# Two of three merge gates by one level of Strassen's scheme, in a decoder layer with fp32 split into two fp32r halves

## The chip, the cores and the metric

One core of a Trainium2 chip. The metric is the device time of one execution in microseconds; lower is better. Engines: TensorE (PE, its weight loads PEld), VectorE (DVE), ScalarE (ACT), GpSimd (POOL), SyncE (SP), and 16 DMA engines.

## The reference, cut to what matters

```
h = rms_norm(x, norm_g)                                  # x: 256 tokens x 1024
(qa, ka, va, ga, ub, vb, gb, qc, gc, ma, mb, mc) = split_cols(h @ w_in, IN_SPLITS)
out_a = moba_attention(rope(qa), rope(ka), va) * silu(ga)          # 6 heads x 128
out_b = gmlp_spatial_gate(ub, vb, ...) * silu(gb)                  # 6 groups x 128
out_c = memory_cross_attention(qc, rms_norm(mem), w_mem_kv) * silu(gc)   # 4 heads x 128
y = (sigmoid(ma) * (out_a @ w_branch_a) + sigmoid(mb) * (out_b @ w_branch_b)
     + sigmoid(mc) * (out_c @ w_branch_c))               # ma, mb, mc: 256 x 1024 each
return rms_norm(x + y @ w_out, final_norm_g)
```

All is fp32. Each of `ma`, `mb`, `mc` is a product of 256x1024 by 1024x1024.

## The kernel before

Every fp32 operand of a matmul is split into two fp32r halves, hi (ScalarE, a copy) and lo = value - hi (VectorE), and a product is three passes: hi hi, hi lo, lo hi (`mm3`).

The weights come as one stream of pieces of 128x2048 (1 MB), loaded by SP into `raw`; half a piece is a chunk. `split(c)` makes chunk c's hi and lo (128x1024 each, four buffers each), three chunks ahead of its use. The loop at the end runs over the chunks in one order: 12 `vvb` (value and gMLP columns), 24 of queries, keys, `ub` and `ga`, 4 `qc`, 4 `mk`, 4 `mv`, 4 `gc`, 6 `gb`, 24 `sig` (the gates: two halves of 512 columns for each of the three, four chunks a half), 16 `br` (branch projections), 8 `out`. A `fea` chunk is 24 matmuls of 256 columns with the weights stationary; a `tok`, `br` or `out` chunk is 12 of 512 columns with the activations stationary. A `sig` half goes from PSUM through ScalarE's sigmoid into `sig0`, `sig1`.

Between the chunks stand units (`U.add`): pieces of the attentions, the norms, the gMLP. `U.slot` takes a unit when those that it follows are done and its costs (PE, DVE, ACT, POOL) fit into the chunk's room. The engines' queues are filled in this written order, and each engine works its own queue from the front.

PSUM has two tags of four banks, `acc` and `aux`. `mm_br` multiplies each branch's accumulators with its gates and adds them up; `y_split` transposes the sum and splits it for the output projection. In the tables below h and `nh`/`nl` are the normalized x, transposed, as hi and lo halves (128 x 8 x 256).

Of the kernel before, what the change touches and what calls it, by code (L numbers as in the profile page):

```python
# [81 lines left out]
def tile_hybrid_layer(ctx: ExitStack, tc: tile.TileContext, xw, memT, mem, x, fin_g, ln_g, w, w_sp, b_sp, rope, out):  # L82
# [14 lines left out]
    def bank():  # L97
        return psum.tile([128, 512], F32, name="aux", tag="aux", bufs=4)

    def acc_bank():  # L100
        return psum.tile([128, 512], F32, name="acc", tag="acc", bufs=4)
# [8 lines left out]
    RAW, SPL, LEAD = 3, 4, 3  # L110
# [167 lines left out]

    def mm3(p, s_hi, s_lo, m_hi, m_lo, first, last):
        nc.tensor.matmul(p, s_hi, m_hi, start=first, stop=False)  # L280
        nc.tensor.matmul(p, s_hi, m_lo, start=False, stop=False)  # L281
        nc.tensor.matmul(p, s_lo, m_hi, start=False, stop=last)  # L282

# [10 lines left out]
    def mm_tok(c):  # L294
# [3 lines left out]
        if k0 == 0:  # L298

            acc[name, o] = [bank(), bank()] if o == 1024 else [acc_bank(), acc_bank()]  # L300
        for i in range(2):
# [14 lines left out]
        if k0 + 2 == KD and name == "vvb":
            U.add(f"ev{o}", lambda: evict_v(o), after=["xrms"], cost=(0, 0, 1.2, 0), gap=1, first=True)
        elif k0 + 2 == KD and name == "sig":
            for t in range(2):
# [2 lines left out]
                nc.scalar.activation(V[f"sig{t}"][:, o, :], acc[name, o][t], AF.Sigmoid)  # L322
# [27 lines left out]
    def mm_fea(c):  # L350
# [559 lines left out]
```

## Time and profile before

| what | value |
|---|---|
| three runs | 332.37, 330.72, 332.83 us (median 332.37) |
| profiled execution, span from the first to the last instruction | 330.5 us (the page gives no other time of it) |
| instructions | 5066 |
| TensorE busy | 322.3 us, 98% |
| VectorE, ScalarE, GpSimd busy | 223.1, 191.7, 39.7 us |
| DMA | 62.91 MB, 190 GB/s in the mean |

A row of a group reads: line, engine, operation, output<-inputs, shapes, count | busy us, mean ns of one | idle us before them and who ended it. A row of the timeline reads: start us, duration us, engine, line, operation. Matmuls overlap, so the distance between starts is their pace.

### The profile page before, as it was taken

What the parts mean: (1) busy time and instruction counts of PE and PEld (TensorE: products, weight loads), DVE (VectorE), ACT (ScalarE), POOL (GpSimd) and SP (SyncE); (2) the same over time, 40 slices, a digit from 0 to 9 for tenths busy, and PEclk for the clock granted to TensorE, in tenths of its full rate; (3) what the DMA queues carried; (4) which work ended last, traced back from release to release, by engine and by line L of the source; (5) the groups of instructions that cost most, each with busy time, mean ns of one, the idle gap of its engine ahead of it and who ended that gap; (6) DMA issues with size and microseconds to landing.
All of it is one profiled execution on the core that took longest, in us unless ns stands there. A gap on an engine that the chain in (4) does not pass through costs nothing.

```text
span 330.5 us, 5066 instructions
## 1 busy us (share of the span) xinstructions
PE 322.3 (98%) x1998; PEld 290.0 (88%) x1998; DVE 223.1 (68%) x339; ACT 191.7 (58%) x315; POOL 39.7 (12%) x42
## 2 busy tenths in 40 slices
PE   7999999999999999999999999999999999999992
PEld 4888899999999999988999988888888888888882
DVE  5864969978957898678694755354435469768553
ACT  5777769566785666547864466535553633533432
POOL 0007310000001090100026530000000000000022
PEclk9999999999999999999999999999999999999997
DMA  7998884554433371643655263646465565563003
GB/s 276 393 420 313 313 346 144 225 183 167 164 139 130 127 255 41 225 138 117 242 190 211 70 236 136 248 153 229 140 243 172 209 184 198 143 238 129 0 4 124
DMA packets 11159, 62.91 MB, mean 190 GB/s; under 512 B 1248, under 2 KB 2400, under 8 KB 4608
## 3 DMA queue, kind: packets, MB, share of 16 engines
q1 hardware_dynamic: 10560, 61.62, 51.8%
q10 hardware_dynamic: 576, 0.98, 0.8%
q8 instruction: 15, 0.25, 0.3%
q14 instruction: 8, 0.07, 0.1%
HBM read 61.55 MB, written 1.05 MB: 189 GB/s over the span
## 4 chain that ended last, share of the span: by engine, by line
PE 96%; DMA 1%; DVE 1%; ACT 0%; issue 0%; DVEq 0%; SPq 0%
PE acc L280 26%; PE acc L281 26%; PE acc L282 26%; PE acc L309 4%; PE aux L280 3%; PE aux L281 3%; PE aux L282 3%; PE aux L472 2%; DMA st<-in_xw_dram 1%; PE aux L641 1%; PE aux L512 0%; PE aux L545 0%; PE aux L226 0%; DVE xk L755 0%; DVE fb L770 0%; ACT jk L760 0%
## 5 line engine op out<-in xcount | busy, mean ns | idle before, releaser
L134 DVE TENSOR_TENSOR lo<-raw,hi 128x1024 fp32r<-128x1024 f32 x102 | 127.7, 1254 | 72.6 <-ACT hi L130 68.4
L130 ACT ACTIVATE hi<-raw 128x1024 fp32r<-128x1024 f32 x102 | 107.7, 1057 | 55.5 <-PE acc L282 47.4
L280 PE MATMUL acc<-nh,hi 128*128 128x256 f32 x304 | 86.7, 285 | 0.0
L282 PE MATMUL acc<-nh,lo 128*128 128x256 f32 x304 | 86.0, 283 | 0.0
L281 PE MATMUL acc<-nl,hi 128*128 128x256 f32 x304 | 86.0, 283 | 0.0
L281 PEld LDWEIGHTS acc<-nl,hi 128*128 128x128 f32 x304 | 58.3, 192 | 0.0
L280 PEld LDWEIGHTS acc<-nh,hi 128*128 128x128 f32 x304 | 58.3, 192 | 0.0
L282 PEld LDWEIGHTS acc<-nh,lo 128*128 128x128 f32 x304 | 58.3, 192 | 0.0
L280 PE MATMUL acc<-hi,nh 128*128 128x512 f32 x96 | 37.5, 390 | 0.0
L282 PE MATMUL acc<-hi,nl 128*128 128x512 f32 x96 | 37.4, 389 | 0.0
L281 PE MATMUL acc<-lo,nh 128*128 128x512 f32 x96 | 37.4, 389 | 0.0
L282 PEld LDWEIGHTS acc<-hi,nl 128*128 128x128 f32 x96 | 18.0, 188 | 3.8
L280 PEld LDWEIGHTS acc<-hi,nh 128*128 128x128 f32 x96 | 18.0, 188 | 3.7
L281 PEld LDWEIGHTS acc<-lo,nh 128*128 128x128 f32 x96 | 18.0, 188 | 3.7
L764 POOL TENSOR_TENSOR xk<-xk,fing 128x512 f32<-128x512 f32 (+1 forms) x4 | 4.0, 1010 | 126.6 <-ACT jk L760 126.6
L650 POOL TENSOR_TENSOR qk<-qk,ga 128x512 f32<-128x512 f32 x3 | 4.0, 1334 | 71.5 <-ACT qk L546 71.5
L421 POOL TENSOR_TENSOR st<-st,bc 128x256 f32<-128x256 f32 x8 | 7.9, 1026 | 25.6 <-DMA trig<-in_rope_dram 25.6
L322 ACT ACTIVATE sig<-acc 128x512 f32<-128x512 f32 x12 | 7.1, 598 | 5.3 <-PE acc L282 4.9
L280 PE MATMUL acc<-hi,ah 128*128 128x512 f32 x24 | 9.4, 393 | 0.0
L282 PE MATMUL acc<-hi,al 128*128 128x512 f32 x24 | 9.4, 390 | 0.0
L281 PE MATMUL acc<-lo,ah 128*128 128x512 f32 x24 | 9.3, 389 | 0.0
L282 PE MATMUL acc<-hi,obl 128*128 128x512 f32 x24 | 9.3, 389 | 0.0
(210 smaller groups left out, 592.3 us busy)
## 6 DMA issues: line engine op xcount, KB each, us to landing
raw<-in_w_dram SPq DMA_DIRECT2D x50, 1024.0 KB, 4.8
st<-in_xw_dram SPq DMA_DIRECT2D x6, 384.0 KB, 6.3
raw<-in_w_dram SPq DMA_DIRECT2D x2, 512.0 KB, 8.6
xk<-in_x_dram SPq DMA_DIRECT2D x1, 1024.0 KB, 11.9
mt<-in_memT_dram SPq DMA_DIRECT2D x2, 512.0 KB, 7.0
mm<-in_mem_dram SPq DMA_DIRECT2D x2, 512.0 KB, 8.6
fing<-in_fin_g_dram SPq DMA_DIRECT2D x1, 512.0 KB, 5.7
out_dram<-xk ACTq DMA_DIRECT2D x2, 224.0 KB, 2.6
```

Source lines behind the costliest of these rows:

```text
L130: nc.scalar.activation(hi[c][:, a:b], raw[c // 2][:, o + a:o + b], AF.Copy)
L134: nc.vector.tensor_tensor(lo[c][:, a:b], raw[c // 2][:, o + a:o + b], hi[c][:, a:b].bitcast(F32), OP.subtract)
L280: nc.tensor.matmul(p, s_hi, m_hi, start=first, stop=False)
L281: nc.tensor.matmul(p, s_hi, m_lo, start=False, stop=False)
L282: nc.tensor.matmul(p, s_lo, m_hi, start=False, stop=last)
L309: nc.tensor.matmul(acc[name, o][t][:, a:b], src[:, k, tsl(t)], wt[c][:, i * 512 + a:i * 512 + b], start=k + n == 0, stop=k == KD - 1 and n ...
L322: nc.scalar.activation(V[f"sig{t}"][:, o, :], acc[name, o][t], AF.Sigmoid)
L421: U.add(f"nm{k}", lambda k=k: nc.gpsimd.tensor_tensor(x_k(k), x_k(k), bc["x"], OP.mult), after=["xrms"], gap=1)
L472: nc.tensor.transpose(p[:, hsl(j)], src, ident)
L641: nc.tensor.matmul(pv[:, a, t, :], V["vb"][:, t, hsl(g)], wsp[:, g, :], start=True, stop=True)
L650: nc.gpsimd.tensor_tensor(src, src, g, OP.mult)
L764: nc.gpsimd.tensor_tensor(z, z, V["fing"][:, a:b], OP.mult)
```

## The change

**The gates a and b.** With h and the weight cut into quarters (tokens by 128, inner and outer columns by 512), each gate is seven products of quarter size in place of eight (Winograd's form of Strassen's scheme): p1 and p2 on quarters of h, p5, p6, p7, p3 on four sums of quarters (`quad_sums`, GpSimd; split into `sh` and `sl` by `quad_hi`, `quad_lo`), p4 on a quarter again. A product is 12 matmuls of 512 columns and splits two tiles of 128x1024. The sums of weight quarters are made by DMA: `base` holds quarter 0, p1 uses it, then quarters 1, 3 and 2 are added to it by accumulating transfers from GpSimd's queue, and p5, p6 and p4 use it; p2, p3 and p7 come through the stream, p7 with one add. The results add up in PSUM (banks x and y, held over several products) and in the gates' tiles. Gate c is computed as before. The sigmoid becomes a tanh of half the value, with the factors folded into `mm_br` and `y_split`.

**The order.** The 14 products stand among 22 ordinary chunks (6 `gb`, the 8 `sig` of gate c, 6 `br` of branch a and 2 of b), by `TURN`. A product counts as two tiles of the four that may be split ahead.

**Banks.** Eight tags of one bank each; `bank()` takes the longest unused one that isn't held, `let_go` gives a held one back.

**Passes.** In a chunk all hi passes stand first and the lo passes follow (`mm_group`, `mm_fea`).

Besides, `raw` has four buffers (before three), x is loaded a second time for the residual, and several tiles share other slots of SBUF.

```diff
-    RAW, SPL, LEAD = 3, 4, 3
+    RAW, SPL = 4, 4
-    for g in range(6):
-        chunks += [("tok", "sig", g, 2 * i) for i in range(4)]
-    for half in range(2):
-        chunks += [("br", half, i) for i in range(KD)]
+    for half in range(2):
+        chunks += [("tok", "sig", half, 2 * i) for i in range(4)]
+    for br, half, n in (("a", 0, HA), ("a", 1, HA), ("b", 0, GB), ("c", 0, HC), ("b", 1, GB), ("c", 1, HC)):
+        chunks += [("br", br, half, k) for k in range(0, n, 2)]
...
+    QUARTER = {"p1": 0, "p2": 2, "p3": 3, "p7": 1}
+    TURN = (0, 0, "p1", 0, "p2", 0, 0, "p5", 0, "p3", 0, 0, "p6", 0, "p7", 0, 0, "p4")
+    n_plain = chunks.index(("fea", "gb", 0))
+    steps, nf = [("F", c) for c in range(n_plain)], n_plain
+    for u in range(2):
+        for p in TURN:
+            steps.append(("S", u, p) if p else ("F", nf))
+            nf += not p
+    ROOM = {"F": (1.3, 1.4, 1.35, 2.5), "S": (1.3, 0.3, 0.5, 2.5)}
...
+    def mm_group(parts):
+        for p, s_hi, s_lo, m_hi, _, first, _ in parts:
+            nc.tensor.matmul(p, s_hi, m_hi, start=first, stop=False)
+            nc.tensor.matmul(p, s_lo, m_hi, start=False, stop=False)
+        for p, s_hi, _, _, m_lo, _, last in parts:
+            nc.tensor.matmul(p, s_hi, m_lo, start=False, stop=last)
...
         for k in range(KD):
-            mm3(p, hi[c][:, hsl(k)], lo[c][:, hsl(k)], sh[:, k, :], sl[:, k, :], k == 0, k == KD - 1)
+            nc.tensor.matmul(p, hi[c][:, hsl(k)], sh[:, k, :], start=k == 0, stop=False)
+            nc.tensor.matmul(p, hi[c][:, hsl(k)], sl[:, k, :], start=False, stop=False)
+        for k in range(KD):
+            nc.tensor.matmul(p, lo[c][:, hsl(k)], sh[:, k, :], start=False, stop=k == KD - 1)
...
+    def quad_sums():
+        V["sx"] = sx = act.tile([128, 4, 4, 128], F32, name="sx", tag="base")
...
+        tt(s1, part(h, 1, 0), part(h, 1, 1), OP.subtract)
+        tt(s1, s1, part(l, 1, 0), OP.add)
...
+    U.add("quads", quad_sums, after=[f"nxl{k}" for k in range(KD)] + ["lna0", "lna1", "mk1"], gap=0)
...
+    def load_base(u):
+        base[u] = act.tile([128, PIECE], F32, name="base", tag="base")
+        nc.gpsimd.dma_start(base[u], quarter(u, 0))
+    def add_quarter(t, u, q):
+        nc.gpsimd.dma_start(t, quarter(u, q), accum_op=OP.add)
...
+    def fast_out(u, p):
...
+        b, i, op = {"p1": (x, 0, None), "p2": (z, 0, OP.add), "p5": (y, 3, None), "p3": (y, 1, None),
+                    "p6": (x, 1, OP.subtract), "p7": (x, 3, OP.subtract), "p4": (x, 2, None)}[p]
+        if p == "p4":
+            tanh_gate(u, 2, x)
+            let_go(("x", u))
+        elif op is None:
+            nc.scalar.activation(GATE[u][i], b, AF.Copy)
...
+        else:
+            nc.vector.tensor_tensor(GATE[u][i], GATE[u][i], b, op)
+            U.add(f"h{u}{i}", lambda: tanh_gate(u, i, GATE[u][i]), cost=(0, 0, 0.65, 0), first=True)
...
+        then = {"p1": 1, "p5": 3, "p6": 2}.get(p)
+        if then is not None:
+            add_quarter(base[u], u, then)
+        if p == "p4" and u < 1:
+            load_base(u + 1)
```

What stands where, at the three places that matter. First TensorE. Before, where the `sig` chunks begin (`mix` is the gMLP's last unit, `wsp,vb`; then per block of 512 columns the passes hi hi, lo hi, hi lo as weight,activation):

```order
L641 MATMUL aux<-wsp,vb 128x128 x4
L280 MATMUL acc<-hi,nh 128x512
L281 MATMUL acc<-lo,nh 128x512
L282 MATMUL acc<-hi,nl 128x512
L280 MATMUL acc<-hi,nh 128x512
L281 MATMUL acc<-lo,nh 128x512
L282 MATMUL acc<-hi,nl 128x512
```

Now the first product, p1 of gate a (L833, whole: two tiles of six matmuls), which stands between the lo passes of gb1 and a transposition of the cross attention:

```order
L393 MATMUL acc<-nh,lo 128x256 x8
L833 MATMUL acc<-hi,nh 128x512
L833 MATMUL acc<-hi,nl 128x512
L833 MATMUL acc<-hi,nh 128x512
L833 MATMUL acc<-hi,nl 128x512
L833 MATMUL acc<-lo,nh 128x512 x2
L833 MATMUL acc<-hi,nh 128x512
L833 MATMUL acc<-hi,nl 128x512
L833 MATMUL acc<-hi,nh 128x512
L833 MATMUL acc<-hi,nl 128x512
L833 MATMUL acc<-lo,nh 128x512 x2
L510 MATMUL acc<-ident,p 128x128 x4
```

A product takes a chunk's place with one chunk's matmuls, and a lo tile is first read by the fifth matmul of its six. 748 matmuls of 512 columns have become 724.

Second, GpSimd from the attention's gating (`qk<-qk,ga`) through the gMLP (`ub`). Before:

```order
L650 TENSOR_TENSOR qk<-qk,ga 128x2x256 x2
L650 TENSOR_TENSOR oc<-oc,gc 128x512
L386 TENSOR_TENSOR ub<-ub,sq 128x256 x2
L689 TENSOR_TENSOR ub<-ub,mt_2192 128x512
L386 TENSOR_TENSOR ub<-ub,sq 128x256
L650 TENSOR_TENSOR oc<-oc,gc 128x512
```

Now, from the last gating of attention on (ahead of it stand the 11 sums, `sx`; L805 is the load of a base, L808 an add):

```order
L688 TENSOR_TENSOR qk<-qk,ga 128x2x256
L805 DMA base<-in_w_dram 128x2048
L688 TENSOR_TENSOR oc<-oc,gc 128x512
L808 DMA base<-in_w_dram 128x2048
L424 TENSOR_TENSOR ub<-ub,sq 128x256 x3
L727 TENSOR_TENSOR ub<-ub,mt_2266 128x512
L808 DMA base<-in_w_dram 128x2048
L424 TENSOR_TENSOR ub<-ub,sq 128x256
L688 TENSOR_TENSOR oc<-oc,gc 128x512
```

An add waits in this queue for the add before it and for VectorE's lo of the tile it adds to; the gatings behind it wait with it.

Third, ScalarE from p6's tiles to p4's (L955 splits a product's tile, L144 a chunk's, `sg` is gate a, `base` and `raw` the tiles split); before, this engine's queue held only chunk splits and sigmoids there:

```order
L955 ACTIVATE hi<-base 128x1024 x2
L144 ACTIVATE hi<-raw 128x1024
L752 ACTIVATE sg_2197<-sg_2197 128x512
L955 ACTIVATE hi<-raw 128x1024 x2
L144 ACTIVATE hi<-raw 128x1024 x2
L752 ACTIVATE sg_2197<-sg_2197 128x512
L955 ACTIVATE hi<-base 128x1024 x2
```

p7's two tiles stand behind the tanh of p6's result (the first L752), p4's behind the tanh of p7's.

More of the change, by code (lines that the diff above doesn't have):

```diff
@@ L95, in slot_tile, with bank, let_go @@
         return V[name]
[L97 to L101, printed above, removed]
+    turn, held = list(range(8)), set()
+    def bank(hold=None):
+        i = next(i for i in turn if i not in held)
+        turn.remove(i)
+        turn.append(i)
+        if hold:
+            held.add(i)
+            V["bank", hold] = i
+        return psum.tile([128, 512], F32, name="acc", tag=f"b{i}")
+    acc_bank = bank
+    def let_go(hold):
+        i = V.pop(("bank", hold))
+        held.discard(i)
+        turn.remove(i)
+        turn.append(i)
     def tsl(t):
@@ L298, in mm_tok @@
         if k0 == 0:
-            acc[name, o] = [bank(), bank()] if o == 1024 else [acc_bank(), acc_bank()]
+            acc[name, o] = [bank((name, o, t) if name != "vvb" else None) for t in range(2)]
         for i in range(2):
@@ new lines, in tile_hybrid_layer, with load_ring @@
+    ring = []
+    for i, stp in enumerate(steps):
+        if stp[0] == "F" and stp[1] % 2 == 1 and stp[1] // 2 >= 2:
+            ring.append((i, stp[1] // 2))
+        elif stp[0] == "S" and stp[2] in ("p2", "p3", "p7"):
+            ring.append((i, stp))
+    ring.sort(key=lambda r: r[0])
+    n_loaded = [2]
+    def load_ring(upto):
+        while n_loaded[0] < len(ring) and ring[max(0, n_loaded[0] - RAW + 1)][0] <= upto:
+            _, what = ring[n_loaded[0]]
+            n_loaded[0] += 1
+            if isinstance(what, int):
+                load(what)
+            else:
+                raw[what] = wts.tile([128, PIECE], F32, name="raw", tag="raw", bufs=RAW)
+                nc.sync.dma_start(raw[what], quarter(what[1], QUARTER[what[2]]))
@@ new lines, in tile_hybrid_layer @@
+    nxt = 4
+    last = at["F", n_br + 4 - 1]
+    for i, stp in enumerate(steps[:last + 1]):
+        now[0] = i
+        U.room = ROOM[stp[0]]
+        U.slot(i, False)
+        while nxt < len(steps) and sum(tiles_of(x) for x in steps[i:nxt + 1]) <= SPL:
+            split_step(steps[nxt])
+            load_ring(nxt)
+            nxt += 1
+        for j in range(i, min(i + 8, len(steps))):
+            nx = steps[j]
+            if nx[0] == "S" and nx[2] == "p7" and nx not in cq and nx in raw and at[nx] - i <= 6:
+                cq[nx] = True
+                add_quarter(raw[nx], nx[1], 3)
+        if stp[0] == "S":
+            mm_fast(*stp[1:])
+            fast_out(*stp[1:])
+        else:
+            c = stp[1]
+            kind = chunks[c][0]
+            if kind == "tok":
+                mm_tok(c)
+            elif kind == "fea":
+                mm_fea(c)
+            elif kind == "br":
+                mm_br(c)
+            else:
+                mm_out(c, 0)
+                for a, b in (((0, 256), (256, 512)) if chunks[c][1] else ((0, 512),)):
+                    mm_out(c, 1, a, b)
+            U.done[f"c{c}"] = i
+        U.slot(i, True)
```

208 lines of the change are left out of this document (144 added, 64 removed).

## The prediction

> **What bounds the kernel now.** I read the page's head first, then the chain of work that ended last, then TensorE's own waits, and last the busy time by stretches.
>
> ```profile
> span 330.5 us, 5066 instructions
> PE 322.3 (98%) x1998; PEld 290.0 (88%) x1998; DVE 223.1 (68%) x339; ACT 191.7 (58%) x315; POOL 39.7 (12%) x42
> PEclk9999999999999999999999999999999999999997
> PE 96%; DMA 1%; DVE 1%; ACT 0%; issue 0%; DVEq 0%; SPq 0%
> ```
>
> TensorE is busy for 98% of the span at an undiminished clock, and 96% of the chain is its own work. A busy PE may still hide short holes, so the waits of that engine alone come next:
>
> ```profile
> PE aux L193 <- DVE warm L183: 1.2, 1, 1.2
> PE acc L309 <- ACT hi L243: 0.6, 2, 0.3
> ```
>
> Both belong to the first microseconds. From there to the last matmul TensorE never waits for a split, a load or a bank. Two things follow. What leaves TensorE shortens the kernel at the matmul's own pace; and letting the lo passes follow the hi passes cannot gain anything by itself, since no lo is waited for now. It can only widen a margin.
>
> **The pace of what goes.** Four starts from the sig chunks, which the change rewrites (start, duration):
>
> ```profile
> 202.84 0.39 PE L280 MATMUL acc<-hi,nh 128*128 128x512 f32 x1
> 203.06 0.39 PE L281 MATMUL acc<-lo,nh 128*128 128x512 f32 x1
> 203.29 0.39 PE L282 MATMUL acc<-hi,nl 128*128 128x512 f32 x1
> ...
> 209.86 0.39 PE L281 MATMUL acc<-lo,nh 128*128 128x512 f32 x1
> ```
>
> Starts are what count, not the 0.39 us. Between the first and the last of these rows are 31 starts in 7.02 us: 0.2265 us each. The step is 0.22 or 0.23 whether the stationary tile is the one of the row before (L280 to L281) or another one (L281 to L282), so the new order of passes should cost and gain nothing here.
>
> Two gates now take 2 x 8 chunks x 12 matmuls = 192; as 2 x 7 products x 12 they take 168. Everything else on TensorE keeps its number: 1144 of 256 columns and 78 of 128 in both programs, 748 of 512 before and 724 after. **Saved: 24 x 0.2265 = 5.4 us**, the most that this change can bring.
>
> **What it puts on VectorE and ScalarE.** Fourteen products split 28 tiles of 1024 columns where sixteen chunks split 16: 12 more on each engine. Results add 3 VectorE adds per gate and 3 more ScalarE copies or tanhs per gate (7 for 4); the four sums need 4 conversions and 4 subtractions; one more table load stands among the gb chunks.
>
> ```profile
> L134 DVE TENSOR_TENSOR lo<-raw,hi 128x1024 fp32r<-128x1024 f32 x102 | 127.7, 1254 | 72.6 <-ACT hi L130 68.4 <-PE acc L281 3.3
> L130 ACT ACTIVATE hi<-raw 128x1024 fp32r<-128x1024 f32 x102 | 107.7, 1057 | 55.5 <-PE acc L282 47.4 <-PE aux L282 5.6 <-DMA raw<-in_w_dram 2.4
> L322 ACT ACTIVATE sig<-acc 128x512 f32<-128x512 f32 x12 | 7.1, 598 | 5.3 <-PE acc L282 4.9
> L731 DVE TENSOR_TENSOR sig<-acc,sig 128x512 f32<-128x512 f32 x12 | 8.0, 683 | 0.0
> L484 ACT ACT_TABLE_LOAD x3 | 3.8, 1283 | 0.0
> 174.00:280.00 106.00, 106.00 (x539) 90.73 (x539) 56.91 (x57) 52.71 (x63) 11.62 (x10) 1.00 0.53 187
> ```
>
> The last row is the stretch from the first gb chunk to the middle of the branches (columns: length, busy us of PE, PEld, DVE, ACT, POOL, clock, DMA share, GB/s). VectorE gets 12 x 1.254 + 6 x 0.683 = 19.1 us on top of 56.9, ScalarE 12 x 1.057 + 6 x 0.598 + 1.283 = 17.6 us on top of 52.7. In the 101 us that remain this is 75% and 70%: there is room on the average. The room is thin where a product follows a product's result. p7's hi stands on ScalarE behind a tanh, which waits for VectorE's subtraction of p6. From p6's end: 0.683 + 0.598 + 1.057 = 2.34 us to the first hi tile, 1.254 more to its lo, 3.59. TensorE has one ordinary chunk meanwhile, 12 x 0.2265 = 2.72, and wants the lo four matmuls later, at 3.62. It just fits; hence I put 0.1 to 0.3 us on each of such places (p2 and p7 of both gates), together 0.5. Were the lo still wanted by the second matmul, as in the old order, the same place would cost 0.7: here the widened margin is used.
>
> **The sums on GpSimd.** The sums of hi and lo quarters are 11 tensor_tensor of 128x512 on POOL. They wait only for tiles that are long there, so they run where POOL comes free, right behind its second gating of attention, far ahead of the chunk that plans them:
>
> ```profile
> 123.19 1.31 POOL L650 TENSOR_TENSOR qk<-qk,ga 128x512 f32<-128x512 f32 x1
> 139.12 1.41 POOL L650 TENSOR_TENSOR qk<-qk,ga 128x512 f32<-128x512 f32 x1 [14.62 <-ACT qk L546]
> 136.61 0.42 DVE L288 TENSOR_TENSOR mkl<-sq,cx 128x256 fp32r<-128x256 f32 x1
> 139.60 1.21 DVE L288 TENSOR_TENSOR mkl<-sq,cx 128x256 fp32r<-128x256 f32 x1
> 185.68 1.29 POOL L689 TENSOR_TENSOR ub<-ub,mt 128x512 f32<-128x512 f32 x1 [0.54 <-DVE mt L646]
> 185.83 2.23 DVE L134 TENSOR_TENSOR lo<-raw,hi 128x1024 fp32r<-128x1024 f32 x1 [0.29 <-ACT hi L130]
> 192.10 1.22 DVE L134 TENSOR_TENSOR lo<-raw,hi 128x1024 fp32r<-128x1024 f32 x1
> 127.00:160.00 33.00, 33.00 (x235) 30.86 (x234) 26.11 (x50) 20.97 (x47) 1.41 (x1) 1.00 0.47 160
> ```
>
> The same VectorE instruction takes 0.42 alone and 1.21 beside a GpSimd one, 1.22 alone and 2.23 beside one: it ends as if it had begun when GpSimd's ended. So 11 x 1.29 = 14.2 us of sums run from about 124.5 to 140 or 150, in the stretch where VectorE has 33.0 - 26.1 = 6.9 us of air, less 4 x 0.68 = 2.7 for the new lo halves: 4.2. The two delayed rows lost 0.79 and 1.01 us; at one such loss for half of the sums, 11 x 0.9 / 2 = 5.0. What the air doesn't take, the lead of the splits takes:
>
> ```profile
> 0.00:133.30 133.30, 49.12 (x40) 1.00 0.62 229
> 0.00:164.20 164.20, 59.00 (x49) 1.00 0.59 216
> 133.29 0.41 DVE L371 TENSOR_TENSOR sq<-acc,bc 128x256 f32<-128x256 f32 x1
> 165.26 0.38 ACT L382 ACTIVATE gc<-acc 128x256 f32<-128x256 f32 x1
> ```
>
> The first two rows count finished splits (chunk 4 is the first). At 133.3, when chunk 40 (mk0) is evicted, chunk 43 is split: three ahead. At 165.26, when chunk 50 (gc2) is evicted, it is chunk 52: only two, some 4 us before it is wanted. So a delay of 5 us should vanish in 4.2 of air and 4 of lead. Bounds: 0 at the low end; at the high end all eleven cost VectorE a full 1.29, and 14.2 - 4.2 - 4 = 6.0 us reach TensorE. I take 0.5.
>
> The Trainium skill, "SBUF — State Buffer", section Who interferes with whom, has this as a rule: a VectorE instruction with two SBUF inputs and a GpSimd one that reads SBUF share a read interface, and the later one blocks fully. The rows above agree (2.23 against 1.22). By it as a worst case, every sum blocking, the 6.0 us hold and the gain is gone; by the share seen in the trace, 0.5.
>
> **The accumulating transfers.** A gate's base tile is loaded, and three times a quarter is added to it by DMA from GpSimd's queue; p7's tile gets one such add. No row shows an accumulating transfer. The nearest:
>
> ```profile
> raw<-in_w_dram SPq DMA_DIRECT2D x50, 1024.0 KB, 4.8
> xk<-in_x_dram SPq DMA_DIRECT2D x1, 1024.0 KB, 11.9
> ```
>
> A plain 1 MB lands in 4.8 us in the steady part, in 11.9 in the crowded start. An add must read what it adds to: I take twice 4.8, 9.6 us, with 4.8 and twice 11.9 = 23.8 as ends. The time there is: the add waits for the split of the product that used the tile, and the next one is split five steps later (p1, p5, p6, p4 are five apart). That is 5 x 2.72 = 13.6 us less the two splits themselves (2 x 1.057 + 1.254 = 3.4): 10.2 until ScalarE would wait, and two steps less one hi (5.4 - 1.1) more, about 14.5, until TensorE would. At 9.6 it is hidden. From p4 to the next gate's p1 are three steps and a plain load: 4.8 until ScalarE waits, 9 until TensorE does, for 4.8. Load on the queues: the stretch moves 11 MB of ordinary pieces and 16 quarters, eight of them adds. With 8 more for the adds' second read that is 35 x 1.05 = 36.7 MB in 101 us, 363 GB/s; 187 GB/s made a share of 0.53, so this is 1.03, full, and without the second reads 0.79. Each of six adds into a base may be late at times; I take no stall, by the nearer row, and leave it as the great risk.
>
> The Trainium skill, "DMA: Bandwidth & Descriptors", section Bandwidth, gives 6.15 us for 1 MB issued from GpSimd; twice that, an estimate, is 12.3 us, and by it TensorE still waits for none.
>
> **Sum.** -5.4 (matmuls) + 0.5 (thin places) + 0.5 (sums) + 0 (adds) = -4.4 us on the span of 330.5: 326.1. The page gives no time of this execution beyond its span; the three runs lie between 330.72 and 332.83, and their median is 1.9 above the span. I keep that: 332.4 - 4.4 = **328.0 us**, 1.3% faster.
>
> **Rivals.** *The sums eat it*: VectorE falls behind before the first product and, with two splits per product, can't catch up. For it speaks the 2.23 row, against it the 4.2 us of air. With 2 to 6 us of stalls: 329 to 333, within 1% of now. *The adds are too slow*: beyond 14.5 us from issue to landing every base add stops TensorE, six times. At 15.4 the gain is gone (6 x 0.9), at 18 it is -4.4 + 6 x 3.5 = +16.6, 349 us; at the bound of 23.8, 384. For it speaks the share near full, against it that plain loads at a share of 0.53 still land in 4.8. *The change doesn't do what it says*: the saved matmuls might run at another pace, as the twelve of a product go into one bank with alternating stationary tiles. The equal steps of 0.22 and 0.23 speak against it; 168 x 0.01 = 1.7 us at most, 329.7.
>
> **Chances.** Forecast with up to 2 us of further stalls (325.3 to 329): 0.55. Gain eaten, by sums, thin places or pace (329 to 335.7): 0.25. Adds or anything else beyond: 0.20. About 1% is what a measurement of this kernel can tell from no change. The range takes in the first two cases: its low end is the fastest run less the whole saving, 330.7 - 5.4 = 325.3; its high end 335.
>
> **What would show it.** Right: TensorE's waits still hold only the start; 24 matmuls of 512 columns fewer at 0.2265; adds landing in under 14 us. The sums: rows of lo splits near 2.2 us between 124 and 150. Wrong: TensorE waiting for ScalarE's or VectorE's splits of base tiles, which in turn wait for the DMA queue of GpSimd; or many lo waits from 150 to 180.

## The result, and the profile after

The changed kernel takes 335.73 us in the median (334.19 to 336.45, four runs), the kernel before 331.56 beside it: a ratio of 1.0105, 95% interval 1.0059 to 1.015 (ratios here are worked out from the single runs; the two medians alone would give 1.0126). It is 1% slower, where 328.0 us, 1.3% faster, had been forecast. In the ratios of the experiments below one slow run each of runs 10 and 17 is left out, while the medians keep it. The profiled run took 335.84 us.

The page of the changed kernel (span; busy time of each engine; the chain that ended last):

```profile
span 334.1 us, 5145 instructions
PE 321.2 (96%) x1974; PEld 287.3 (86%) x1974; DVE 251.6 (75%) x361; ACT 206.9 (62%) x338; POOL 66.0 (20%) x62
PE 69%; DVE 16%; ACT 8%; issue 3%; DMA 1%; POOL 1%; DVEq 0%; SPq 0%; ACTq 0%; POOLq 0%
```

TensorE has less to do and a longer span. What it waited for (us in total, times, longest us), the waits of the first microseconds set aside (L207, 1.3, and L342, 0.5):

```profile
PE acc L510 <- DVE p L533: 2.4, 3, 1.2
PE acc L393 <- DVE lo L148: 1.1, 1, 1.1
PE acc L833 <- ACT hi L955: 0.9, 1, 0.9
```

Three waits in the middle of the program, none of which stood in the profile before, and their places by windows (length, then busy us of PE, PEld, DVE, ACT, POOL, clock, DMA share, GB/s):

```profile
120.00:140.00 20.00, 17.84 (x136) 17.45 (x135) 16.97 (x29) 9.66 (x23) 19.53 (x12) 0.91 0.39 143
133.00:136.40 3.40, 3.40 (x19) 3.40 (x18) 3.40 (x6) 1.08 (x2) 3.32 (x3) 0.51 0.69 246
170.00:200.00 30.00, 29.73 (x221) 27.97 (x220) 24.73 (x28) 21.01 (x35) 8.54 (x9) 1.00 0.56 161
200.00:240.00 40.00, 37.90 (x180) 31.19 (x179) 29.80 (x27) 23.90 (x30) 9.97 (x9) 1.00 0.90 274
```

Before, TensorE was busy for the whole of the first, third and fourth of these. The first, before:

```profile
120.00:140.00 20.00, 20.00 (x169) 19.94 (x169) 15.67 (x31) 11.29 (x27) 5.38 (x4) 1.00 0.47 159
```

Two places carry the loss: 120 to 140 us, long before the first product, where GpSimd is busy for 19.53 of 20 us, and 200 to 240 us, among the products of gate a.

To count it whole, take the time from each matmul's start to the next beyond the pace of its kind (0.2266, 0.1195 and 0.061 us for 512, 256 and 128 columns), and sum it by stretch. I call this the loss.

| stretch, us | before | after |
|---|---|---|
| 0 to 10 | 4.14 | 4.79 |
| 10 to 120 | 2.10 | 2.19 |
| 120 to 150 | 0.97 | 4.75 |
| 150 to 170 | 0.66 | 0.46 |
| 170 to 200 | 1.28 | 1.94 |
| 200 to 240 | 0.01 | 3.41 |
| 240 to the end | 0.90 | 1.37 |
| start of the last matmul | 323.87 | 327.28 |

The losses grow by 8.85 us. The saved matmuls, 24 x 0.2266, take 5.44 off; what is left is the 3.41 us by which the last matmul starts later.

**120 to 150 us.** The timeline (start, us, what, idle before and its releaser), from GpSimd, VectorE and TensorE:

```profile
125.20 1.34 POOL L764 TENSOR_TENSOR sx<-nh 128x512 f32<-128x512 f32 x1
126.62 2.16 POOL L765 TENSOR_TENSOR sx<-sx,nl 128x512 f32<-128x512 f32 x1
...
142.05 1.35 POOL L773 TENSOR_TENSOR sx<-sx,nl 128x512 f32<-128x512 f32 x1
125.31 2.31 DVE L148 TENSOR_TENSOR lo<-raw,hi 128x1024 fp32r<-128x1024 f32 x1
130.06 1.56 DVE L533 TENSOR_SCALAR p<-p,rc 128x128 f32<-128x128 f32 x2
130.40 0.33 PE L510 MATMUL acc<-ident,p 128*128 128x128 f32 x1 [1.21 <-DVE p L533]
131.68 0.44 PE L510 MATMUL acc<-ident,p 128*128 128x128 f32 x2 [0.95 <-DVE p L533]
```

The sums run from 125.2 to 143.4. The lo split takes 2.31 us, as forecast, but TensorE doesn't wait for it. It waits for `p`, the normalised probabilities of attention, which it transposes one chunk later: their two instructions take 1.56 us (0.55 in a stretch without GpSimd), after the 2.31 us of the split ahead of them. The profile before held a sign of this: beside the gating of attention at 123.19 the same pair took 1.94 us there, without a stop of TensorE, and the next pair 0.55:

```profile
122.71 1.94 DVE L495 TENSOR_SCALAR p<-p,rc 128x128 f32<-128x128 f32 x2
127.80 0.55 DVE L495 TENSOR_SCALAR p<-p,rc 128x128 f32<-128x128 f32 x2
```

After the two stops the granted clock stands at 0.51 for 3.4 us.

**200 to 222 us.** First the wait for `lo` in a gb chunk:

```profile
198.30 0.89 POOL L808 DMA_DIRECT2D base<-in_w_dram  x1 [3.74 <-DVE lo L956]
198.91 1.06 POOL L424 TENSOR_TENSOR ub<-ub,sq 128x256 f32<-128x256 f32 x1
199.61 1.60 POOL L688 TENSOR_TENSOR oc<-oc,gc 128x512 f32<-128x512 f32 x1
200.86 1.59 POOL L727 TENSOR_TENSOR ub<-ub,mt 128x512 f32<-128x512 f32 x1
202.12 1.02 POOL L424 TENSOR_TENSOR ub<-ub,sq 128x256 f32<-128x256 f32 x1
198.59 5.65 DVE L148 TENSOR_TENSOR lo<-raw,hi 128x1024 fp32r<-128x1024 f32 x1
204.28 1.22 PE L393 MATMUL acc<-nh,lo 128*128 128x256 f32 x8 [1.15 <-DVE lo L148]
```

The add waits 3.74 us for a lo split, and GpSimd's queue behind it. Then four multiplications run back to back, and a split of 1.22 us takes 5.65: it ends as if it had begun when the last of them (203.14) was done. Next, p7 of gate a:

```profile
215.65 1.89 DVE L697 TENSOR_TENSOR obl<-ub,obh 128x512 fp32r<-128x512 f32 x3
218.59 0.68 DVE L852 TENSOR_TENSOR sg<-sg,acc 128x512 f32<-128x512 f32 x1
219.31 0.63 ACT L752 ACTIVATE sg<-sg 128x512 f32<-128x512 f32 x1 [3.42 <-DVE sg L852]
219.85 1.99 ACT L955 ACTIVATE hi<-raw 128x1024 fp32r<-128x1024 f32 x2
220.94 0.50 PE L833 MATMUL acc<-hi,sh 128*128 128x512 f32 x1 [0.89 <-ACT hi L955]
```

ScalarE stands 3.42 us at the tanh, p7's hi tiles behind it; the subtraction that the tanh needs stands on VectorE behind three conversions of the gMLP (1.89 us) and a split.

**The adds** themselves did what was forecast: 8.0, 10.0 and 12.0 us from issue to landing (least, median, most), against 9.6 taken; TensorE never waits for one, ScalarE a little:

```profile
DMA to landing us min/median/max: 8.0/10.0/12.0
ACT hi L955 <- DMA base<-in_w_dram: 4.2, 3, 2.4
```

### The profile page after: what moved, and what is told of

Same layout as the page of the kernel before. It is cut to its first block, busy times and chain, and to the rows that moved or that the text cites. A ratio compares the mean times of both kernels' runs of the same rounds, so it can differ in the third digit from the quotient of the medians.

```text
span 334.1 us, 5145 instructions
## 1 busy us (share of the span) xinstructions
PE 321.2 (96%) x1974; PEld 287.3 (86%) x1974; DVE 251.6 (75%) x361; ACT 206.9 (62%) x338; POOL 66.0 (20%) x62
## 3 DMA queue, kind: packets, MB, share of 16 engines
HBM read 70.98 MB, written 1.05 MB: 216 GB/s over the span
## 4 chain that ended last, share of the span: by engine, by line
PE 69%; DVE 16%; ACT 8%; issue 3%; DMA 1%; POOL 1%; DVEq 0%; SPq 0%; ACTq 0%; POOLq 0%
PE acc L313 10%; PE acc L315 10%; PE acc L312 10%; PE acc L393 8%; PE acc L391 8%; PE acc L390 8%; PE acc L833 7%; DVE lo L148 6%; PE acc L342 4%; DVE lo L956 2%; ACT p L522 2%; ACT hi L955 2%; ACT hi L144 1%; DVE nm L517 1%; DMA st<-in_xw_dram 1%
## 5 line engine op out<-in xcount | busy, mean ns | idle before, releaser
L144 ACT ACTIVATE hi<-raw 128x1024 fp32r<-128x1024 f32 x86 | 89.5, 1054 | 14.0 <-PE acc L313 11.5
L393 PE MATMUL acc<-nh,lo 128*128 128x256 f32 x304 | 42.8, 283 | 1.1 <-DVE lo L148 1.1
L393 PEld LDWEIGHTS acc<-nh,lo 128*128 128x128 f32 x304 | 39.2, 192 | 1.3 <-DVE lo L148 1.3
L956 DVE TENSOR_TENSOR lo<-base,hi 128x1024 fp32r<-128x1024 f32 x16 | 18.9, 1221 | 13.4 <-ACT hi L955 13.4
L955 ACT ACTIVATE hi<-base 128x1024 fp32r<-128x1024 f32 x16 | 16.0, 1048 | 4.2 <-DMA base<-in_w_dram 4.2
L752 ACT ACTIVATE sg<-sg 128x512 f32<-128x512 f32 x6 | 3.8, 632 | 19.0 <-DVE sg L852 19.0
L833 PE MATMUL acc<-hi,sh 128*128 128x512 f32 x32 | 12.8, 400 | 0.9 <-ACT hi L955 0.9
L312 PE MATMUL acc<-hi,yh 128*128 128x512 f32 (+1 forms) x40 | 13.6, 349 | 0.0
L313 PE MATMUL acc<-hi,yl 128*128 128x512 f32 (+1 forms) x40 | 13.6, 347 | 0.0
L808 POOL DMA_DIRECT2D base<-in_w_dram x6 | 5.3, 889 | 39.4 <-DVE lo L956 39.4
L312 PE MATMUL acc<-hi,hh 128*128 128x512 f32 x32 | 12.5, 392 | 0.0
L833 PE MATMUL acc<-hi,sl 128*128 128x512 f32 x32 | 12.5, 391 | 0.0
```

The lines of the kernel that those rows point to most:

```text
L144: nc.scalar.activation(hi[c][:, a:b], raw[c // 2][:, o + a:o + b], AF.Copy)
L313: nc.tensor.matmul(p, s_lo, m_hi, start=False, stop=False)
L393: nc.tensor.matmul(p, lo[c][:, hsl(k)], sh[:, k, :], start=False, stop=k == KD - 1)
L833: nc.tensor.matmul(b, a, m[:, o:o + 512], start=n == 0 and p in ("p1", "p2", "p5"), stop=n == 11, skip_group_check=p in ("p6", "p7", "p4", ...
L955: nc.scalar.activation(hi[j], part, AF.Copy)
L956: nc.vector.tensor_tensor(lo[j], part, hi[j].bitcast(F32), OP.subtract)
```

## The experiments

The theory has three parts: T1, the sums in a row on GpSimd hold up VectorE, and through it the attention; T2, what gathers behind a waiting add runs as a burst that does the same; T3, the tanh holds up p7's hi. The rivals stand with each run. Results are medians, ratios to the kernel before on the same chip with 95% intervals, and the losses, in us, of three stretches (after the change: 4.75, 1.94, 3.41; before: 0.97, 1.28, 0.01). The stretches are fixed times, while the kernels shift by a few us.

| kernel | us | ratio | 120-150 | 170-200 | 200-240 |
|---|---|---|---|---|---|
| 1 without the sums | 333.52 | 1.0029 (1.0007-1.0051) | 2.59 | 2.98 | 2.05 |
| 2 sums on VectorE | 333.04 | 1.0022 (1.0001-1.0044) | 0.90 | 4.77 | 2.93 |
| 3 adds later | 337.63 | 1.0156 (1.0122-1.0191) | 4.75 | 1.29 | 5.83 |
| 4 tanh later | 335.83 | 1.0114 (1.0092-1.0137) | 3.25 | 2.80 | 2.91 |
| 5 plain loads for adds | 333.45 | 1.005 (1.0027-1.0074) | 4.74 | 1.64 | 3.12 |
| 6 old order of passes | 339.70 | 1.0219 (1.0185-1.0253) | 3.26 | 3.63 | 5.44 |
| 7 before, lo passes last | 332.27 | 1.0 (0.9977-1.0023) | 0.96 | 1.29 | 0.01 |
| 8 = 2, gatings on VectorE | 333.00 | 1.0015 (0.9995-1.0035) | 0.89 | 3.75 | 2.84 |
| 9 = 8, tanh later | 331.25 | 0.9972 (0.995-0.9994) | 0.92 | 3.75 | 1.67 |
| 10 = 9, p1 of b from the ring | 331.82 | 0.9992 (0.9963-1.0022) | 0.91 | 3.74 | 1.31 |
| 11 = 9, splits first | 330.90 | 0.9957 (0.9935-0.9979) | 0.92 | 3.09 | 1.59 |
| 12 = 10 and 11 | 330.13 | 0.9953 (0.9925-0.9981) | 0.92 | 3.09 | 0.72 |
| 13 sums early on GpSimd | 335.05 | 1.0092 (1.0062-1.0122) | 0.90 | 4.78 | 2.87 |
| 14 = 12, sums early on GpSimd | 332.40 | 1.0025 (0.9997-1.0052) | 0.92 | 2.87 | 1.13 |
| 15 = 12, sums back | 332.14 | 1.0012 (0.9988-1.0035) | 2.76 | 1.28 | 1.56 |
| 16 = 12, gatings back | 332.47 | 1.0005 (0.9982-1.0028) | 0.91 | 3.78 | 1.08 |
| 17 sums on VectorE, order kept | 332.19 | 1.0001 (0.9969-1.0032) | 0.76 | 2.95 | 2.01 |
| 18 = 12, sums as in 17 | 328.00 | 0.9861 (0.9824-0.9898) | 0.69 | 1.73 | 0.04 |

### 1 and 2: the sums left out, the sums on VectorE

```diff
-        tt(s1, part(h, 1, 0), part(h, 1, 1), OP.subtract)
...
+        for s in (s1, s2, s3, s4):
+            nc.gpsimd.memset(s, 0.0)
```

> The ten quarter sums on GpSimd are left out (four GpSimd fills of the same tiles stand in their place, so the conversions, subtractions and products that follow still run, on zeros). T1 (the sums hold up VectorE, and through it the transposes of the attention's probabilities): TensorE loses nothing between 120 and 140 us, its clock stays at full there, and 3.9 us go: 335.7 - 3.9 = 331.8, within 331 to 332.5. Rival R1 (the loss at 120 to 140 comes from the new rotation of PSUM banks or the new order of the lo passes): the stalls stay, 335 to 336. Rival R2 (the sums cost only their 0.95 + 1.21 us of waits, and the low clock is chance): 333.5.

```diff
+    for n in range(10):
+        U.add("quads" if n == 9 else f"quads{n}", lambda n=n: quad_sum(n), gap=1,
+              after=[f"quads{n - 1}"] if n else [f"nxl{k}" for k in range(KD)])
```

> The same ten sums, on VectorE, one per chunk from about chunk 14 on instead of all in a row on GpSimd. T1: VectorE spends 10 x 0.64 = 6.4 us more, spread over ten chunks in which it is not the bound, and GpSimd holds it up no more: about as without the sums, 331.8 (331 to 333). Rival R1 (banks or passes): 335 to 336. Rival R3 (VectorE has no room for the sums on any engine): lo splits late from 60 to 100 us, TensorE waits there, 335 or more.

The first gained 2.2 us of the 3.9 expected. Its four fills are no neutral stand-in: beside a gating and them `p` took 3.79 us, and TensorE stopped once, for 1.21 instead of 1.21 and 0.95 us. The time is the 333.5 of R2, but with one of the two stops still there the run can't tell T1 from R2. The second says it clearly for 120 to 150 (loss 0.90, as before the change), against R1. But its time is at the edge of what T1 allows, since 170 to 200 lost 4.77 in place of 1.94: TensorE waited for `p` of the cross attention, and for the hi of p2's tiles. Part of what was gained was given back later. Why, runs 17 and 18 show.

### 3 and 4: the adds later, the tanh later

```diff
-            add_quarter(base[u], u, then)
+            late.append((now[0] + 2, base[u], u, then))
```

> The adds into a base tile are issued two steps later in the program, so that the gMLP's gatings and other GpSimd work no longer stand behind an add in its queue. T2 (an add that waits for a lo split holds GpSimd's queue, and what gathers behind it then runs as one burst that keeps VectorE from its next split for 5.65 us): the gap of 1.36 us at 203 goes, no VectorE row over 4 us stands in the gb chunks, 335.7 - 1.5 = 334.2 (333.5 to 334.7). Rival R4 (the gap at 203 has another cause): 335.7. Rival R5 (the adds now land too late): ScalarE and TensorE wait for base tiles, 336 to 345.

```diff
-            U.add(f"h{u}{i}", lambda: tanh_gate(u, i, GATE[u][i]), cost=(0, 0, 0.65, 0), first=True)
+            tanhs.append(lambda: tanh_gate(u, i, GATE[u][i]))
...
+        while tanhs:
+            tanhs.pop(0)()
```

> The tanh of the results of p2, p6 and p7 is issued behind the splits of its step on ScalarE instead of ahead of them. T3 (ScalarE waits 3.42 us for p6's subtraction with the hi of p7's tiles behind that tanh): the stalls around p7 of both gates, 1.2 + 0.9 us and the paced gaps around them, shrink to under 0.7 together: 335.7 - 2 = 333.7 (332.5 to 334.5). Rival R6 (p7's tiles are late on VectorE or by DMA, not behind the tanh): 335.7, with the same gaps.

Each removed its own stall and paid elsewhere. With later adds the wait at 203 went (T2), but the adds then came too late (R5, 336 to 345 us): ScalarE waited 7.0 us for base tiles in place of 4.2, and TensorE lost 1.50 us ahead of one (its matmul starts at 229.95). With the later tanh the stop ahead of p7 went (T3), and ScalarE, no longer held there, came to the base tiles before the adds had landed. Its waits in that run, to be held against the 4.2 us above:

```profile
ACT hi L955 <- DMA base<-in_w_dram: 17.7, 5, 5.9
```

So the tanh's delay and the adds' landing lay beside each other: taking away one alone uncovered the other, and the time is R6's 335.7 without R6's reason. In this run TensorE's two stops at 130 us are the same as in the changed kernel, but the clock held:

```profile
133.00:136.40 3.40, 3.40 (x31) 3.40 (x30) 3.40 (x6) 1.17 (x3) 3.32 (x3) 1.00 0.79 248
```

31 matmul records in place of 19, loss 3.25 instead of 4.75: the slow stretch takes 1.5 us there and comes in some executions only. Its 1.5 us are not seen in the end, though. Where the clock held, the transposes of attention at 157 and 183 us were waited for longer (losses of 0.35 and 1.31 us, in the changed kernel only one of 0.43, at 183), and from 120 to 200 us the two profiles lose the same, 7.17 and 7.15 us.

### 5: plain loads in place of the adds

```diff
-        nc.gpsimd.dma_start(t, quarter(u, q), accum_op=OP.add)
+        nc.gpsimd.dma_start(t, quarter(u, q))
```

> The kernel after the change with its eight accumulating transfers as plain loads of the same megabyte in the same place (the weight quarters are thus not summed). T4 (the adds' landing of 8 to 12 us lies beside other work, as forecast): they land in 5 to 7 us, ScalarE's 4.2 us of waits for base tiles go, TensorE gains nothing: 335.7, within 0.8. Rival R8 (the adds' second read of memory slows the loads around them and starves the splits from 200 us on): 333.5 or less, with no gap at 219 and 270.

```profile
DMA to landing us min/median/max: 5.1/5.2/6.6
```

The price of accumulating is 10.0 against 5.2 us for the same megabyte from the same queue. TensorE keeps all its stalls (the loss from 10 us on falls by 0.76), as T4 says, and R8's sign, no gap at 219, did not come (1.05 lost at 218). Yet the median is 2.3 us lower than after the change, which is R8's time; the intervals of the two ratios overlap. Part of the difference is the first 10 us (2.76 lost in this profile, 4.79 in the other; see the end). Whether the adds cost anything beyond that, this run doesn't settle.

### 6 and 7: the order of the passes, taken back and alone

```diff
-            passes += [(2 * (k // 2), a_hi, hi[j], o), (2 * (k // 2), a_lo, hi[j], o), (2 * (k // 2) + 1, a_hi, lo[j], o)]
-        passes.sort(key=lambda x: x[0])
+            passes += [(0, a_hi, hi[j], o), (0, a_hi, lo[j], o), (0, a_lo, hi[j], o)]
```

> The kernel after the change with the old order of passes (hi hi, hi lo, lo hi per pair of tiles) everywhere outside the first chunks. T5 (the new order buys each thin place some 0.7 us): the waits for lo grow at 129, 203, 220 and 270, 335.7 + 2 = 337.7 (336.7 to 339). Rival R9 (the order of the passes is worth nothing): 335.7, within 0.6.

```diff
+        for p, s_hi, s_lo, m_hi, _, first, _ in parts:
+            nc.tensor.matmul(p, s_hi, m_hi, start=first, stop=False)
+            nc.tensor.matmul(p, s_lo, m_hi, start=False, stop=False)
+        for p, s_hi, _, _, m_lo, _, last in parts:
+            nc.tensor.matmul(p, s_hi, m_lo, start=False, stop=last)
```

> The kernel before with one part of the change alone: the lo passes behind all hi passes of a pair of tiles; no Strassen, no sums, old banks. T5 (the order buys time only where a lo tile is late, and before the change none is): 332.4, within 0.6. Rival R10 (the order by itself changes the matmuls' pace, by up to 0.005 us for each of some 1150 matmuls): 327 to 331 or 334 and more.

In the changed kernel the order is worth 4.0 us, twice what T5 gave it (the loss at 204 alone grows from 1.30 to 2.16). The slow clock doesn't explain the difference, since both profiles hold one such stretch: run 6's stands not at 133 but behind the stop at 204.

```profile
205.00:208.40 3.40, 3.40 (x19) 3.40 (x18) 3.38 (x3) 0.67 (x1) 0.00 (x0) 0.51 0.98 207
```

In the kernel before it is worth nothing: an order that makes room for a late tile pays only where one is late.

### 8 and 9: the gatings on VectorE, and the tanh later on top

```diff
-            nc.gpsimd.tensor_tensor(V["ub"][:, h, :], V["ub"][:, h, :], g, OP.mult)
+            U.add(f"gbm{h}", lambda: nc.vector.tensor_tensor(V["ub"][:, h, :], V["ub"][:, h, :], g, OP.mult),
+                  after=[f"gb{h}"], gap=1, first=True)
```

> The sums on VectorE as before (333.0 us alone), and besides the gatings of attention, cross attention and gMLP from the second on (14 multiplications) on VectorE too, so that from 140 us on GpSimd issues only the base loads and adds. T2 (a burst of GpSimd work behind an add holds up VectorE): the stalls of 1.49 us at 178, 1.36 at 184 and 0.81 at 202 of the kernel with the sums alone go or fall under 0.4 each, and no VectorE row between 170 and 230 is longer than its kind needs by over 0.5 us: 333.0 - 2.7 = 330.3 (329.3 to 331.3). Rival R7 (VectorE is short of time itself; the gatings only change engine): 333 or more, with lo waits between 175 and 230.

> The kernel with sums and gatings on VectorE, and the tanh of p2, p6 and p7 behind the splits. Alone the tanh's move took the 1.05 us gap ahead of p7 of gate a and gave it back as waits of ScalarE for base tiles (17.7 us in place of 4.2) and new gaps at 236 and 270. T3a (the adds were late because their lo splits were held by GpSimd's bursts): with the bursts gone both gains hold, 1.5 below the kernel without the move: 328.8. Rival T3b (the adds' landing of 10 us itself now binds, whatever stands on GpSimd): within 0.7 of the kernel without the move, 330.3, with TensorE waiting for hi of base tiles.

Of the three stalls named, 178 fell from 1.49 to 0.37 and 202 went, but the one at 184 stayed (1.45): T2 was wrong there. The time of 333.0 misses the 330.3 and is R7's, but without the waits for lo that R7 names: TensorE now stopped at 225 and 234 for hi of base tiles, so once more the adds came into the open. With the tanh later as well, 1.75 us went (forecast: 1.5), where alone it had gained nothing. That is T3a, and this kernel is the first below the kernel before.

### 10 to 12: p1 of gate b from the ring, the splits first, both

```diff
-        return raw["S", u, p] if p in ("p2", "p3", "p7") else base[u]
+        return raw["S", u, p] if p in ("p2", "p3", "p7") or (u, p) == (1, "p1") else base[u]
```

> The kernel with sums and gatings on VectorE and late tanh (331.25), and gate b's p1 from a tile of the ring that is loaded ahead, while the base tile gets its load and first add at the same time (one megabyte more is moved). T6 (from p4 of gate a to p1 of gate b the base load has too little time): ScalarE's waits for base tiles around 227 to 237 go, the losses of 0.86 + 0.34 us there fall under 0.3: 330.3. Rival R11 (the megabyte more makes other tiles late): 331.3 or more.

```diff
-        U.slot(i, False)
+        early = at["S", 0, "p1"] <= i <= at["S", 1, "p4"]
+        if not early:
+            U.slot(i, False)
         while nxt < len(steps) and sum(tiles_of(x) for x in steps[i:nxt + 1]) <= SPL:
...
+        if early:
+            U.slot(i, False)
```

> The same kernel of 331.25 with the splits of a step ahead of the evictions and conversions of other work on ScalarE and VectorE, from the first product of gate a to the last of gate b. T7 (p2's hi of gate a starts late because the conversion of the gated cross attention, 0.63 us and 0.44 us of waiting, stands ahead of it on ScalarE): the stall of 1.45 us at 183 falls to 0.4, 331.25 - 1.1 = 330.2. Rival R12 (the work behind the splits is then late itself): 331.2 or more.

> Both edits on the kernel of 331.25: if T6 and T7 hold and add up, 331.25 - 0.9 - 1.1 = 329.2 (328.6 to 330), 1% below the kernel before. By R11 and R12: 331.2 or more.

The ring alone missed: 331.82, which is R11's time, and ScalarE still waits 16.4 us for base tiles (18.5 without the ring). The splits first removed the stall at 183 as T7 said. TensorE's wait, first without and then with them:

```profile
PE acc L832 <- ACT hi L954: 1.2, 1, 1.2
```

```profile
PE acc L832 <- ACT hi L954: 0.2, 1, 0.2
```

The time fell by 0.35 us only, less than such runs can tell; with both edits it was 330.13, just above the 328.6 to 330 forecast.

### 13 and 14: the sums on GpSimd, but early

```diff
-    U.add("quads", quad_sums, after=[f"nxl{k}" for k in range(KD)] + ["lna0", "lna1", "mk1"], gap=0)
+    U.add("quads", quad_sums, after=[f"nxl{k}" for k in range(KD)], gap=0)
```

> The kernel after the change with its ten sums still in a row on GpSimd, but as soon as their inputs are there (some 60 us earlier, beside nothing but the splits of ordinary chunks and a little set-up). T1a (the place decides: lo splits have two to three chunks of lead, the attention's normalisation has none): lo splits of over 2 us there, TensorE loses nothing by them, nor between 120 and 140: 335.7 - 3.5 = 332.2 (331.5 to 333). Rival R13 (fourteen us of GpSimd reads hold up VectorE so long that any place costs the same): 335 to 336, with waits for lo between 50 and 90 us.

> The best kernel so far (gatings on VectorE, late tanh, gate b's p1 from the ring, splits first; 330.13) with the sums early on GpSimd in place of VectorE. T1a: within 0.7 of 330.1. Rival R13: 333 or more.

Here the sums run from 35.5 to 55.6 us, beside lo splits and set-up, in the changed kernel:

```profile
41.61 3.28 POOL L766 TENSOR_TENSOR sx<-sx,nl 128x512 f32<-128x512 f32 x1 [2.42 <-DVE nl L248]
...
37.97 2.31 DVE L148 TENSOR_TENSOR lo<-raw,hi 128x1024 fp32r<-128x1024 f32 x1
41.39 2.35 DVE L148 TENSOR_TENSOR lo<-raw,hi 128x1024 fp32r<-128x1024 f32 x2
54.41 2.32 DVE L148 TENSOR_TENSOR lo<-raw,hi 128x1024 fp32r<-128x1024 f32 x1
```

Two splits of 2.3 us here too (the 2.35 at 41.39 are two ordinary ones, and there it is the sum that waits, 3.28 us), and yet TensorE's only wait for a lo tile between 20 and 70 us is one of 0.5; the loss from 10 to 60 rises by 1.2 us, where in the change's own place it rose by 3.8. So the lead of the splits does work, and by the loss the place decides most of the price. The times are nearer to R13 all the same, because what was won at 120 to 150 was lost again at 170 to 200 (4.78), as in run 2. The fair comparison is with run 2, which has every other instruction in the same order: early sums on GpSimd cost 2.0 us more than sums on VectorE in the median, and in the best kernel 2.3, 1.1 of them from 10 to 60. That lies between the two theories.

### 15 and 16: one thing put back

In the best kernel so far (12) the sums, then the gatings, back where the change had them.

> The best kernel (330.13) with one thing put back: the ten sums in a row on GpSimd in the place that the change gave them. T1 (they cost 2.6 us of stalls there, with a slow-clock stretch up to 4): stalls at the transposes of the attention's probabilities between 120 and 140 us, 330.1 + 2.6 to 4 = 332.7 to 334.1. Rival R14 (the sums only took time that other stalls would have taken): 330.1, within 0.7.

> The best kernel (330.13) with one thing put back: the gatings on GpSimd, behind the adds in its queue. T2 (what gathers behind a waiting add runs as one burst and holds up VectorE): VectorE rows over 3 us between 175 and 215, TensorE waiting for splits there, 330.1 + 1.5 to 2.5 = 331.6 to 332.6. Rival R15 (the other edits give the splits enough lead): 330.1, within 0.7.

The sums brought back their stalls at the transposes (0.70 and 1.23 us), and 2.0 us, less than the 2.6 to 4 expected; at the same time the cross attention moved back, and the loss at 170 to 200 fell from 3.09 to 1.28. The gatings brought back 2.3 us, but not by the long burst. That is there again, a split of 5.03 us, but with the splits first TensorE doesn't wait for it; the stall, a loss of 1.49 us, stands some 15 us earlier, at the end of a chain of short delays. In the rows, VectorE's `nm` is late beside GpSimd's `ub`, ScalarE waits for `nm` and TensorE for `p`; the last row is the long split:

```profile
175.27 1.38 DVE L517 TENSOR_SCALAR nm<-mx 128x2 f32<-128x2 f32 x1
175.53 1.08 POOL L424 TENSOR_TENSOR ub<-ub,sq 128x256 f32<-128x256 f32 x1
176.72 1.28 ACT L522 ACT_TABLE_LOAD   x1 [1.84 <-DVE nm L517]
179.68 0.81 PE L510 MATMUL acc<-ident,p 128*128 128x128 f32 x4 [1.33 <-DVE p L533]
...
194.85 5.03 DVE L148 TENSOR_TENSOR lo<-raw,hi 128x1024 fp32r<-128x1024 f32 x1
```

An instruction on 128x2, 0.17 us alone, takes 1.38 beside a gating, and the transposes behind the exponentials are late by as much.

### 17 and 18: the sums on VectorE, everything else in its place

In run 2 the sums were done earlier, so the planner moved their conversions, and with them the cross attention, a chunk up. Here the last sum is given the old condition; apart from the sums, every engine has the changed kernel's order.

```diff
-              after=[f"quads{n - 1}"] if n else [f"nxl{k}" for k in range(KD)])
+              after=[f"quads{n - 1}"] + (["lna0", "lna1", "mk1"] if n == 9 else []) if n else [f"nxl{k}" for k in range(KD)])
```

> The kernel after the change with its ten sums on VectorE, one per chunk, and every other instruction of every engine in the order that it has there (in the earlier run with the sums on VectorE the cross attention had moved up with them). T1 (the sums on GpSimd hold up VectorE and cost 2.6 us of stalls and 1.2 to 1.5 us of slow clock between 120 and 150): the loss there falls from 4.75 to 0.9, nothing is lost again at 170 to 200, 335.7 - 3.85 = 331.9 (331.2 to 332.6). Rival R16 (a stall that goes from 120 to 150 turns up again behind, wherever the cross attention stands): 333 to 334.

> The best kernel with the sums on VectorE and the cross attention where the change had put it. By the other runs 0.9 us is lost between 120 and 150, 1.3 between 170 and 200 (3.1 in the best kernel so far): 330.1 - 1.8 = 328.3 (327.6 to 329.3), 1.2% below the kernel before. Rival R16: 330 or more.

```profile
L769 DVE TENSOR_TENSOR sx<-sx,nl x6: 671/678/684, 46.9 to 137.8; 128x512 f32<-128x512 f32 x6
120.00:140.00 20.00, 20.00 (x169) 19.91 (x169) 16.27 (x33) 11.84 (x26) 5.37 (x4) 1.00 0.48 176
```

A sum takes 0.68 us on VectorE (1.27 to 2.35 on GpSimd), and TensorE is busy throughout. 332.19 us: **the sums' place cost 3.5 us** by the medians, give or take 2 by the intervals of the two ratios, and 4.0 by the loss from 120 to 150. That only makes the kernel as fast as the one before (ratio 1.0001). The thin places of the products stay as they were: 5.35 us lost from 170 to 240 after the change, 4.96 here. R16 falls.

The best kernel so built takes 328.0 us, 1.4% less than the kernel before (ratio 0.9824 to 0.9898; six runs, 326.4 to 329.7). It is run 15's kernel with nothing moved but the sums, and so a second measure of their place: 332.14 less 328.00, 4.1 us. The page and TensorE's waits of the profiled run, which took 329.7 us and is the slowest of the six:

```profile
span 328.0 us, 5136 instructions
PE 318.3 (97%) x1974; PEld 285.4 (87%) x1974; DVE 248.2 (76%) x384; ACT 206.7 (63%) x338; POOL 32.6 (10%) x39
```

```profile
PE acc L832 <- ACT hi L954: 1.3, 1, 1.3
```

One stall over 0.3 us is left after the first ten, at 263 us: p7's tile of gate b, whose add was issued at 250.4 and for which ScalarE waits 5.62 us.

## Why the prediction failed

Two terms of the sum failed: the sums on GpSimd and the thin places, 0.5 us each in the forecast. By the loss they measured 3.8 and 4.5.

- **The matmuls saved**: right. The pace held (0.2266), so 5.44 us went; the rival that the saving isn't there falls. (Matmuls of 128 columns are 106 in both traces, not 78; the saving doesn't hang on it.)
- **The sums, 0.5 us: the first step that failed.** "What the air doesn't take, the lead of the splits takes" holds for splits nearly throughout: in their own place TensorE waited for none, in run 13 once, for 0.5 us. But the step looked only at splits. In that stretch VectorE also normalises the attention's probabilities, which TensorE transposes in the next chunk, where the splits are two to three chunks ahead; that chain broke first. Measured: 3.8 us of loss, 1.5 of them in the slow clock after the stops (3.4 us at 0.51), and 3.5 and 4.1 us in the medians when the sums alone move (runs 17 and 18). The upper bound of 6.0 covers the size, but was worked out for the splits. The sums are ten, too, and not eleven; at 1.27 to 2.35 us apiece they still filled 18 us.
- **The thin places, 0.5 us: the second, and the larger miss.** 4.5 us (170 to 240: 5.35 less 1.29; 240 on: 0.47). Only some 2 us of it lie where the prediction looked, at p7: 1.5 in gate a and 0.4 in gate b. "It just fits" gave p7's hi 2.34 us from p6's end; in truth the subtraction stood behind 1.89 us of gMLP conversions and a split, and ScalarE waited 3.42 us. Most of the rest lies outside the products: 1.4 us at 204, in a gb chunk, and 0.4 us at 183, at a transpose of probabilities. The term priced its places each by itself, without GpSimd: the burst behind the waiting add (5.65 for 1.22) was not in the sum at all. Runs 3 and 8 take the stop at 204 away, run 4 the one ahead of p7, and run 18 has neither.
- **The adds**: 9.6 us taken, 10.0 measured, hidden in this kernel. Its note that ScalarE would wait beyond 10.2 us was right as well; runs 4, 8 and 9 show that it becomes the next bound as soon as the other delays go.
- **The pass order**: the margin counted on for p7 is real: 4.0 us in the whole kernel (run 6), by which the forecast would have been missed further.
- **The rest**, 0.65 us, is the first ten microseconds, which differ among executions of any of these kernels.
- **The rivals**: "the sums eat it" named the right work and engine, at 329 to 333 us, but not the way. It had VectorE fall behind until the products and not catch up; in fact 150 to 170 us lose no more than before (0.46 against 0.66). The Trainium skill, "SBUF — State Buffer", section Who interferes with whom, has it that a VectorE instruction with two SBUF inputs contends with a GpSimd one that reads SBUF, and that the later of two that contend blocks for the whole of the other. The splits agree (2.31 us); so does `p`, which has one tensor input only but is of the kind for which the section names modes that use the shared ports (0.55 alone, 1.56 beside sums, 3.79 beside a gating and fills). Prices for a chain of several GpSimd instructions it doesn't state; here 5.65.

That the best kernel takes the 328.0 us forecast is not the prediction come true: it is another arrangement of the same change, and its forecast (328.3) was made from the runs before it.

The rotation of the PSUM banks was not tried by itself; runs 17 and 18 have it and show no loss of their own from it.

## What to carry to other kernels

When work goes to an engine that holds up another, look for that other engine's work with the shortest lead, not for its most frequent: here the sums cost 3.5 us beside a normalisation of 0.55 us with little lead, and 2.0 beside splits of 1.2 us with two chunks of lead. An instruction that waits in a queue turns the work behind it into a burst; before you place a wait, ask whom that burst will meet. And take stalls away together: alone, a later tanh and later adds gained nothing or lost, and in the kernel without the others' stalls the same tanh gained 1.75 us.

## What the runs showed of the hardware that I had not expected

A waiting VectorE instruction is held through a row of GpSimd instructions, not through one: 5.65 us for 1.22, and even 128x2 elements take 1.38 us for 0.17.

The granted clock fell to 0.51 for 3.4 us after 2.2 us of stops within 3 us, in three profiles of kernels with the sums in their place (after the change, runs 3 and 5), and did not in two others with the same stops (runs 4 and 6). Run 6 shows it later, behind a single stop of 2.00 us. What decides between the two isn't shown.

The start differs among executions. From 4 to 9 us, after the change and in run 12:

```profile
4.00:9.00 5.00, 4.50 (x12) 3.53 (x13) 3.01 (x7) 2.77 (x7) 0.00 (x0) 1.00 0.99 360
```

```profile
4.00:9.00 5.00, 4.24 (x19) 3.15 (x19) 3.63 (x8) 3.08 (x7) 0.00 (x0) 1.00 1.02 354
```

In the one, matmuls of 512 columns start 0.43 us apart until 10.2 us, in the other 0.23 apart from 5.7 us on; the losses of the first ten us are 4.1 to 4.9 or 2.6 to 2.8 (3.6 once). The column of the granted clock shows 1.00 in both, so these rows don't tell the cause. The Trainium skill, "TensorE: Matmul & The Clock Gate", Part 1, says that the first matmuls run at half the clock until a window of some 3.4 us has been busy, and that the count varies from run to run; the 0.43 and 0.23 agree. The start makes some 2 us of scatter that no edit here touches, and it is why the losses were compared from 10 us on.
